# Gated DeltaNet layer of a decoder trunk: triangular inverse on 32- and 64-wide array tiles, decay rows by DRAM

## The chip, the cores and the metric

The kernel runs on one core of a Trainium2 chip. The metric is the device time of one execution in microseconds (us). The core has five engines with an instruction queue each: PE (matrix products; its weight loads are listed apart as PEld), DVE (vector), ACT (scalar functions), POOL (GpSimd) and SP (which here only issues DMAs). An engine works its queue in order.

## The reference

Four residual layers (mixers Mamba-2, HGRN2, Gated DeltaNet, Mamba-2), each followed by cross-attention into 256 memory tokens and a gated MLP; width 1024, 256 tokens, all float32. The change touches the third layer's mixer alone: 8 key heads, 16 value heads of 128, chunks of 64 tokens. Its core, shortened:

```
gc = cumsum(g)                                   # log decay within a chunk
decay = exp(where(incl, gc[l] - gc[s], -inf))
m = where(strict, (k * beta) @ k.T * decay, 0)
a_mat = m + I
sol = triangular_solve(a_mat, [v * beta, k * beta * exp(gc)])   # unit lower triangular
u, w = sol
att = (q @ k.T) * decay
per chunk: v_new = u - w @ state
           o = (q * exp(gc)) @ state + att @ v_new
           state = state * exp(gc_last) + (k * exp(gc_last - gc)).T @ v_new
```

## The kernel before

Tokens are handled as two chunks of 128, so a key head with its two value heads has four 128x128 triangular matrices (index `a`, two value heads by two chunks). All matrices of weights are float32 and are multiplied as three float32r products: `prep` (L152) loads a 128x1024 piece `raw` over SP's queue (four buffers), ACT casts it to `wH` (L160), DVE subtracts to get `wL` (L161), and `mm3` (L166) issues three matmuls with 256 moving columns for each 128x128 block. These projections fill PE. In the DeltaNet layer their outputs are `gps` (input projection, six column blocks a head) and `acc` (output projection).

The work of the heads is written as generators (`head`, L906) that are woven into this stream: `Weave` keeps a clock of PE time; each `yield cost, latency` adds the cost and says how much later the next step may stand. So the position of a step in PE's queue is set when the program is built, not on the chip. Up to three heads are under way at once.

One head does the following. It normalises q and k (`l2`, `kq`), broadcasts two rows of summed log decay over 128 partitions by a matmul with a selector (`grb`, L925: two float32r matmuls with 256 columns), forms the decays `E` (L930 to L933), the products `gp` (L942) and the scaled, masked matrices `MT` (L948) and `att`. `MT` goes to DRAM and its thirty-two 16x16 diagonal blocks come back as `blk` (L956, L957, both on SP's queue). POOL inverts these blocks in fifteen steps (L969, L971) and writes them by DMA into zeroed DRAM (L973); SP loads them as `U`, which is block diagonal (L987). That load stands in SP's queue among the loads of `raw`, and waits there until POOL's write has landed.

The inverse is then grown from blocks of 16 to 32 to 64 to 128. `U` is the transposed inverse, `Tm` the inverse. Four transposes make `Tm` from `U` (`tps`, L993). For each of two levels DVE masks `MT` to `ml` (L964), four 128x128 products give `yps` (L1000), ACT copies them to `Y` (L1005), four more give `ups` (L1009), DVE subtracts from `Tm` (L1011), four transposes (L1015) and an ACT copy (L1016) bring `U` up to date. The last level uses 64x64 products (L1021, L1028). A float32 product shows in the trace as two instructions (passes), a transpose or a float32r product as one. After this the head solves and runs the recurrence (`gvp`, `gsp`, `gs`, `grp`, `gop`, L1037 to L1087), normalises (`token_norm`) and transposes out (`gbp`, L1091).

## Time and profile before

| | |
|---|---|
| median of 3 runs | 2039.09 us (2039.07 to 2043.4) |
| the profiled execution | 2039.35 us |
| its span in the profile | 2037.6 us |
| DeltaNet mixer within the span | about 980 to 1288 us |
| PE busy, whole span | 98% |

The span is the time from the first to the last recorded instruction; 1.75 us of the profiled execution lie outside it. Busy time of PE counts a matmul from its start to the end of its passage through the array, and successive ones overlap, so what PE can deliver is read from the distance between starts, not from the busy share.

### The profile page before, as it was taken

The numbers are of one execution on the slowest core, as the hardware profiler recorded it, in microseconds if no ns is written. First come the engines' busy times: TensorE is split into PE (matmuls) and PEld (weight loads), VectorE is DVE, ScalarE is ACT, GpSimd is POOL, SyncE is SP. The second block draws the span as 40 slices with busy tenths as digits, with TensorE's granted clock in tenths as the row PEclk, the third lists the DMA queues.
The fourth block names the chain that finished last, engine by engine and source line by source line (L and its number), as shares of the span: only waits on it lengthen the run. The fifth ranks groups of instructions, "written<-read, shape, count | busy, mean of one in ns | idle before, by whom it ended". The sixth has DMA issues, their size and how long they took to land.

```text
span 2037.6 us, 42013 instructions
## 1 busy us (share of the span) xinstructions
PE 1987.2 (98%) x17020; PEld 1942.3 (95%) x17020; DVE 1575.0 (77%) x2417; ACT 1280.4 (63%) x1874; POOL 341.6 (17%) x468
## 2 busy tenths in 40 slices
PE   8999999999999999999999999999999999999997
PEld 8999999999999899999998899999999999999997
DVE  6899777875788778866786875878756999777875
ACT  6687666654565566555676875666545778666553
POOL 2032211000133110001064451110001133201001
PEclk9999999999999999999999999999999999999999
DMA  7655545666644546666544333457666565545663
GB/s 242 202 186 173 174 146 167 216 193 181 211 156 135 150 133 211 200 192 192 188 123 136 107 111 123 140 162 217 193 177 200 196 197 171 179 136 176 195 193 121
DMA packets 112770, 351.53 MB, mean 173 GB/s; under 512 B 15744, under 2 KB 25664, under 8 KB 112576
## 3 DMA queue, kind: packets, MB, share of 16 engines
q1 hardware_dynamic: 106176, 333.42, 52.9%
q10 hardware_dynamic: 6144, 15.17, 2.2%
q8 instruction: 133, 2.18, 0.4%
q0 software_dynamic: 256, 0.26, 0.1%
q14 instruction: 61, 0.50, 0.1%
HBM read 344.81 MB, written 4.00 MB: 171 GB/s over the span
## 4 chain that ended last, share of the span: by engine, by line
PE 78%; issue 5%; DVE 5%; ACT 4%; POOL 2%; DMA 1%; DVEq 0%; SPq 0%; POOLq 0%; ACTq 0%
PE ffps L170 8%; PE ffps L169 8%; PE ffps L168 8%; PE acc L168 6%; PE acc L169 6%; PE acc L170 6%; PE mps L168 4%; PE mps L170 3%; PE mps L169 3%; DVE wL L161 2%; PE qps L170 2%; PE qps L168 2%; PE qps L169 2%; PE kvps L168 1%; PE kvps L170 1%
## 5 line engine op out<-in xcount | busy, mean ns | idle before, releaser
L161 DVE TENSOR_TENSOR wL<-raw,wH 128x1024 fp32r<-128x1024 f32 (+2 forms) x639 | 786.3, 1232 | 326.8 <-ACT wH L160 324.3
L160 ACT CAST wH<-raw 128x1024 fp32r<-128x1024 f32 (+2 forms) x639 | 658.9, 1032 | 535.6 <-PE ffps L169 160.8
L168 PE MATMUL ffps<-hH,wH 128*128 128x256 f32 x1376 | 380.6, 277 | 0.0
L169 PE MATMUL ffps<-hL,wH 128*128 128x256 f32 x1376 | 379.8, 276 | 0.0
L170 PE MATMUL ffps<-hH,wL 128*128 128x256 f32 x1376 | 379.2, 276 | 0.0
L168 PE MATMUL acc<-aH,wH 128*128 128x256 f32 x1232 | 344.5, 280 | 0.0
L170 PE MATMUL acc<-aH,wL 128*128 128x256 f32 x1232 | 341.4, 277 | 0.6 <-DVE wL L161 0.6
L169 PE MATMUL acc<-aL,wH 128*128 128x256 f32 x1232 | 341.0, 277 | 0.0
L169 PEld LDWEIGHTS ffps<-hL,wH 128*128 128x128 f32 x1376 | 258.3, 188 | 0.1
L168 PEld LDWEIGHTS ffps<-hH,wH 128*128 128x128 f32 x1376 | 258.3, 188 | 0.1
L170 PEld LDWEIGHTS ffps<-hH,wL 128*128 128x128 f32 x1376 | 258.0, 188 | 0.0
L168 PEld LDWEIGHTS acc<-aH,wH 128*128 128x128 f32 x1232 | 231.5, 188 | 1.3 <-issue 0.7
L170 PEld LDWEIGHTS acc<-aH,wL 128*128 128x128 f32 x1232 | 231.3, 188 | 1.1 <-DVE wL L161 1.0
L169 PEld LDWEIGHTS acc<-aL,wH 128*128 128x128 f32 x1232 | 231.6, 188 | 0.6
L168 PE MATMUL mps<-hH,wH 128*128 128x256 f32 x768 | 218.0, 284 | 0.0
L169 PE MATMUL mps<-hL,wH 128*128 128x256 f32 x768 | 213.8, 278 | 0.0
L170 PE MATMUL mps<-hH,wL 128*128 128x256 f32 x768 | 213.0, 277 | 0.0
L212 POOL TENSOR_TENSOR ns<-nsq 128x256 f32<-128x256 f32 x13 | 10.7, 821 | 856.7 <-ACT nsq L209 856.7
L168 PEld LDWEIGHTS mps<-hH,wH 128*128 128x128 f32 x768 | 144.3, 188 | 2.9 <-issue 2.4
L169 PEld LDWEIGHTS mps<-hL,wH 128*128 128x128 f32 x768 | 144.4, 188 | 0.7
L170 PEld LDWEIGHTS mps<-hH,wL 128*128 128x128 f32 x768 | 144.4, 188 | 0.3
L170 PE MATMUL gps<-hH,wL 128*128 128x256 f32 x448 | 127.6, 285 | 0.6 <-DVE wL L161 0.6
(410 smaller groups left out, 4670.1 us busy)
## 6 DMA issues: line engine op xcount, KB each, us to landing
raw<-f_up SPq DMA_DIRECT2D x176, 512.0 KB, 4.1
raw<-m_in SPq DMA_DIRECT2D x96, 512.0 KB, 3.6
raw<-f_down SPq DMA_DIRECT2D x80, 512.0 KB, 4.2
raw<-xa_kv SPq DMA_DIRECT2D x60, 512.0 KB, 4.3
raw<-g_in SPq DMA_DIRECT2D x48, 512.0 KB, 4.1
raw<-m_out SPq DMA_DIRECT2D x32, 512.0 KB, 3.6
raw<-xa_q SPq DMA_DIRECT2D x32, 512.0 KB, 3.6
raw<-xa_o SPq DMA_DIRECT2D x32, 512.0 KB, 3.6
```

The costliest lines, as they stand in the source:

```text
L160: ACT.copy(H[:, c], raw[:, c])
L161: DVE.tensor_tensor(out=L[:, c], in0=raw[:, c], in1=f32(H[:, c]), op=ALU.subtract)
L168: PE.matmul(dst, aH, bH, start=start, stop=False, skip_group_check=True)
L169: PE.matmul(dst, aH, bL, start=False, stop=False, skip_group_check=True)
L170: PE.matmul(dst, aL, bH, start=False, stop=stop, skip_group_check=True)
L212: self.eng.tensor_tensor(out=self.sum, in0=sq[:, :T], in1=sq[:, T:], op=ALU.add)
```

## The change

The masks, the full-width products and the transposes of the two lower levels go. Products are now made only where blocks are: `MT`, `U` and `Tm` are cut into four groups of 32 partitions, and `block` (L1004 of the changed kernel) issues one small float32 product for each 32-partition group, so a product occupies a 32x32 tile of the array. `Tm` becomes a 128x4x64 tile and holds each half's 64x64 inverse in its own partitions; it is no longer made by transposing `U`. POOL makes a transposed copy of the inverted 16x16 blocks (`ut`), writes it to a third DRAM scratch, and SP loads `Tm` from there with two DMAs a head. Per head the two lower levels are: 16 products with 16 moving columns into `yps`, 12 and 16 products into `ups`, then 8 and 12 products of 32x32. The column `low`, zero or one by partition, takes the place of the mask. ACT writes pieces of `U` and DVE pieces of `Tm` straight from PSUM. The 64x64 level stays as it is.

The broadcast matmul `grb` goes too. The summed log decay rows `pk` are written to DRAM once (`grow`) on ACT's queue and each head's two rows are read back over 128 partitions by one DMA on ACT's queue, issued one head ahead (`fetch`).

By instruction counts over the eight heads: 96 transposes, 128 products of 128x128 and 16 of the broadcast leave PE; 512 small products come (128 with 32 weight columns and 16 moving, 96 of the same form, 128 with 16 and 16, 160 of 32x32). DVE loses 16 masks, 16 subtractions of 128x512 and 8 of 64x256, and gets 24 of 32x64 elements, 16 operations of 32x128 and 8 of 64x256. ACT loses 40 copies of 128x512 and gets 8 activations of 128x64, 48 of 16 or 32 partitions, 8 copies of 32x128 and 8 more loads of a function table. POOL gets 8 copies and 8 DMAs, SP 16 loads of `Tm` and 2 of zeros, ACT's queue 8 reads and 1 write of rows.

The core of the diff:

```diff
-            d = [[dr.tile([4, P + 1, P], F32, name=f"gd{i}{j}") for j in range(2)] for i in range(2)]
+            d = [[dr.tile([4, P + 1, P], F32, name=f"gd{i}{j}") for j in range(2)] for i in range(3)]
             for j in range(2):
-                nc.sync.dma_start(out=rows(d[1][j]), in_=zt)
+                for i in (1, 2):
+                    nc.sync.dma_start(out=rows(d[i][j]), in_=zt)
...
-            gcm = U1([P, 768], "gcm")
-            nc.scalar.dma_start(out=gcm, in_=io["cm"][:, CM["lvl"]:CM["lvl"] + 768])
+            gcm = U1([P, 512], "gcm")
+            nc.scalar.dma_start(out=gcm, in_=io["cm"][:, CM["i16"]:CM["i16"] + 512])
+            lvl, low = U1([P, P], "glvl"), U1([P, 1], "glow")
+            nc.scalar.dma_start(out=lvl, in_=io["cm"][:, CM["lvl"]:CM["lvl"] + P])
+
+            DVE.tensor_reduce(out=low, in_=lvl, axis=AX.X, op=ALU.max)
+            DVE.tensor_scalar(out=low, in0=low, scalar1=-1.0, scalar2=1.0, op0=ALU.mult, op1=ALU.add)
...
-                zero(rw)
-                DVE.tensor_copy(rw[:16], pk[:16])
-                DVE.tensor_tensor(out=rw[32:48], in0=pk[:16], in1=f32(rw[:16]), op=ALU.subtract)
+                nc.scalar.dma_start(out=rows_d, in_=pk[:16])
+
+            rbs = {}
+
+            def fetch(h):
+
+                rbs[h] = wk.tile([P, 2, T], F32, tag="grb", name="grb")
+                nc.scalar.dma_start(out=rbs[h], in_=bass.AP(tensor=rows_d.tensor, offset=rows_d.offset + 2 * h * T,
+                                                             ap=[[0, P], [T, 2], [1, T]]))
+
+            fetch(0)
 
             def columns():
                 tp = mx("gtp")
...
-                rb = mx("grb")
-                for j in range(2):
-                    hv = 2 * h + j
-                    PE.matmul(rb[:, j * T:(j + 1) * T], sel[:, hv:hv + 1].to_broadcast([P, P]), rw,
-                              start=j == 0, stop=True, skip_group_check=True)
+                rb = rbs[h]
+                if h < 7:
+                    fetch(h + 1)
...
-                ACT.activation(out=er, in_=rb.rearrange("p (j t) -> p j t", j=2)[:, :, P:], func=AF.Exp, scale=-1.0)
+                ACT.activation(out=er, in_=rb[:, :, P:], func=AF.Exp, scale=-1.0)
...
                 tm = wk.tile([32, 16, 16], F32, tag="tm", name="tm", bufs=1)
-                d0, d1 = scr[0][h % 2], scr[1][h % 2]
+                ut = wk.tile([32, 16, 16], F32, tag="ut", name="ut", bufs=1)
+                d0, d1, d2 = [s[h % 2] for s in scr]
                 nc.sync.dma_start(out=rows(d0), in_=MT)
...
-                ml = W(f"ml{h % 2}", 1)
-
-                def level(l):
-                    DVE.tensor_tensor(out=ml, in0=MT, in1=lvl[:, l:l + 1, :].to_broadcast([P, 4, P]), op=ALU.mult)
-
-                POOL.tensor_copy(ub.rearrange("p a b -> p (a b)"), gcm[:32, 256:512])
+                POOL.tensor_copy(ub.rearrange("p a b -> p (a b)"), gcm[:32, :256])
                 for j in range(15):
...
                 nc.gpsimd.dma_start(out=diag(d1), in_=ub)
+                POOL.tensor_copy(ut, ub.rearrange("p a b -> p b a"))
+                nc.gpsimd.dma_start(out=diag(d2), in_=ut)
...
                 nc.sync.dma_start(out=U, in_=rows(d1))
-                level(0)
+
+                Tm = wk.tile([P, 4, 64], F32, tag="Tm", name="Tm", bufs=2)
+                for b in (0, 64):
+                    nc.sync.dma_start(out=Tm[b:b + 64], in_=d2[:, b:b + 64, b:b + 64].rearrange("a s l -> s a l"))
                 yield 0, LAT[1]
-
-                tps = mx("tps")
+                Q = [slice(32 * i, 32 * i + 32) for i in range(4)]
+                quad = lambda ps, o, w: ps[:, o:o + 4 * w].rearrange("p (a b) -> p a b", a=4)
+
+                def block(d, lhsT, rhs, first):
+                    PE.matmul(d, lhsT, rhs, start=first, stop=True, skip_group_check=True)
+
+
+                ps = mx("yps")
+                yp = quad(ps, 0, 16)
                 for a in range(4):
-                    PE.transpose(tps[:, a * P:(a + 1) * P], U[:, a, :], ident)
-                Tm = W("Tm")
-                ACT.copy(flat(Tm), tps)
-                yield 440, LAT[2]
-                for l in range(2):
-                    yp = mx("yps")
-                    for a in range(4):
-                        PE.matmul(yp[:, a * P:(a + 1) * P], ml[:, a, :], Tm[:, a, :], start=a == 0, stop=True,
-                                  skip_group_check=True)
-                    if l == 0:
-                        level(1)
-                    Y = W("Y", 1)
-                    ACT.copy(flat(Y), yp)
-                    yield 870, LAT[3]
-                    up = mx("ups")
-                    for a in range(4):
-                        PE.matmul(up[:, a * P:(a + 1) * P], U[:, a, :], Y[:, a, :], start=a == 0, stop=True,
-                                  skip_group_check=True)
-                    DVE.tensor_tensor(out=flat(Tm), in0=flat(Tm), in1=up, op=ALU.subtract)
-                    yield 870, LAT[4]
-                    tps = mx("tps")
-                    for a in range(4):
-                        PE.transpose(tps[:, a * P:(a + 1) * P], Tm[:, a, :], ident)
-                    ACT.copy(flat(U), tps)
-                    yield 440, LAT[14]
-
-                yp = mx("yps")
+                    for i, q in enumerate(Q):
+                        block(yp[q, a], MT[q, a, q], Tm[q, a, 32 * (i % 2):32 * (i % 2) + 16], a == 0)
+                Y = wk.tile([P, 4, 16], F32, tag="Y0", name="Y0", bufs=1)
+                ACT.activation(out=Y, in_=yp, func=AF.Copy, scale=low)
+                yield 300, 1200
+                ps = mx("ups")
+                tp, up = quad(ps, 0, 16), quad(ps, 64, 16)
                 for a in range(4):
-                    PE.matmul(yp[64:, a * 64:(a + 1) * 64], MT[:64, a, 64:], Tm[:64, a, :64], start=a == 0, stop=True,
-                              skip_group_check=True)
-                Y = W("Y", 1)
-                ACT.copy(Y[64:, :, :64], yp[64:, :T].rearrange("p (a b) -> p a b", a=4))
-                yield 440, LAT[3]
-                up = mx("ups")
+                    for q in Q[:3]:
+                        block(tp[q, a], U[q, a, q], Y[q, a], a == 0)
                 for a in range(4):
-                    PE.matmul(up[:64, a * 64:(a + 1) * 64], Y[64:, a, :64], U[64:, a, 64:], start=a == 0, stop=True,
-                              skip_group_check=True)
-                DVE.tensor_tensor(out=U[:64, :, 64:], in0=U[:64, :, 64:], in1=up[:64, :T].rearrange("p (a b) -> p a b", a=4),
-                                  op=ALU.subtract)
-                yield 440, LAT[13]
+                    for i, q in enumerate(Q):
+                        block(up[32 * i:32 * i + 16, a], Y[q, a], U[q, a, 32 * i + 16:32 * i + 32], a == 0 and i == 3)
+                for i in (0, 2, 1):
+                    d = Tm[Q[i], :, 32 * (i % 2):32 * (i % 2) + 16]
+                    DVE.tensor_tensor(out=d, in0=d, in1=tp[Q[i]], op=ALU.subtract)
+                for i in (1, 3, 0, 2):
+                    ACT.activation(out=U[32 * i:32 * i + 16, :, 32 * i + 16:32 * i + 32], in_=up[32 * i:32 * i + 16], func=AF.Copy,
+                                   scale=-1.0)
+                yield 600, 1800
+
+                ps = mx("yps")
+                yp = quad(ps, 0, 32)
+                for a in range(4):
+                    for b in (0, 2):
+                        block(yp[Q[b + 1], a], MT[Q[b], a, Q[b + 1]], Tm[Q[b], a, :32], a == 0)
+                Y = wk.tile([P, 4, 32], F32, tag="Y1", name="Y1", bufs=1)
+                ACT.copy(Y[Q[1]], yp[Q[1]])
+                DVE.tensor_copy(Y[Q[3]], yp[Q[3]])
+                yield 300, 1200
+                ps = mx("ups")
+                tp, up = quad(ps, 0, 32), quad(ps, P, 32)
+                for a in range(4):
+                    block(tp[Q[1], a], U[Q[1], a, Q[1]], Y[Q[1], a], a == 0)
+                    for b in (0, 2):
+                        block(up[Q[b], a], Y[Q[b + 1], a], U[Q[b + 1], a, Q[b + 1]], a == 0)
+                DVE.tensor_scalar(out=Tm[Q[1], :, :32], in0=tp[Q[1]], scalar1=-1.0, scalar2=None, op0=ALU.mult)
+                for b in (2, 0):
+                    ACT.activation(out=U[Q[b], :, Q[b + 1]], in_=up[Q[b]], func=AF.Copy, scale=-1.0)
+                yield 400, 1500
+
...
```

PE's queue in the middle of the layer, with the inverses of two heads interleaved; `tps` are transposes, `yps` and `ups` the two products of a level, `l` and `grb` belong to the next head. Before:

```order
L1015 MATMUL tps<-ident,Tm 128x128 x4
L1000 MATMUL yps<-Tm,ml_13319 128x128 x4
L912 MATMUL l_13651<-gsq,ones 128x512
L925 MATMUL grb<-grw,sel 128x256 x2
L1000 MATMUL yps<-Tm,ml_13019 128x128 x4
L1009 MATMUL ups<-Y,U 128x128 x4
L170 MATMUL gps<-hH,wL 128x256
```

The same part of the layer in the changed kernel:

```order
L1004 MATMUL yps<-Tm,MT 64x64 x4
L168 MATMUL gps<-hH,wH 128x256
L169 MATMUL gps<-hL,wH 128x256
L170 MATMUL gps<-hH,wL 128x256
L168 MATMUL gps<-hH,wH 128x256
L169 MATMUL gps<-hL,wH 128x256
L1004 MATMUL ups<-Y_13732,U 32x16 x12
L1004 MATMUL ups<-U,Y_13732 16x16 x16
L923 MATMUL l_13814<-gsq,ones 128x512
L1004 MATMUL ups<-U,Y 64x64 x4
L1004 MATMUL yps<-Tm,MT 32x32 x8
```

Groups of four large products and of four transposes have become groups of 8 to 28 small ones, and the group of `grb` is gone. By the built program's tile sizes PE goes from 128-wide work to 32-wide tiles 38 times and back 40 times (two of the groups follow 64-wide ones).

SP's queue over the first two heads; the numbers behind `gd` tell scratch tensors apart. Before:

```order
L987 DMA U<-gd_12451 128x4x128
L159 DMA raw<-g_in 128x1024
L956 DMA gd_12450<-MT 128x4x128
L957 DMA blk<-gd_12450 32x16x16
L159 DMA raw<-g_in 128x1024 x3
L987 DMA U<-gd_12452 128x4x128
```

Now:

```order
L994 DMA U<-gd_12450 128x4x128
L966 DMA gd_12449<-MT 128x4x128
L998 DMA Tm<-gd_12452 64x4x64 x2
L967 DMA blk<-gd_12449 32x16x16
L159 DMA raw<-g_in 128x1024 x3
L994 DMA U<-gd_12451 128x4x128
L998 DMA Tm<-gd_12453 64x4x64 x2
```

Behind each load of `U` stand two of `Tm`, which wait for POOL's second write, and between the loads of `U` of these two heads there are three loads of `raw` instead of four.

## Rows read from the trace of the kernel before

**Rows 1.** The page's first part: busy time, share and instructions by engine.

```profile
PE 1987.2 (98%) x17020; PEld 1942.3 (95%) x17020; DVE 1575.0 (77%) x2417; ACT 1280.4 (63%) x1874; POOL 341.6 (17%) x468
```

**Rows 2.** Busy time by stretch, granted clock, DMA: the whole mixer, and ten microseconds in it.

```profile
980.40:1287.50 307.10, 294.87 (x2399) 278.45 (x2398) 229.48 (x433) 220.19 (x330) 117.81 (x269) 0.99 0.41 129
```

```profile
1070.00:1080.00 10.00, 6.81 (x33) 6.52 (x34) 4.67 (x8) 3.00 (x5) 4.74 (x15) 0.66 0.73 247
```

**Rows 3.** PE groups by line, 950 to 1400 us: count | busy, mean ns | idle before.

```profile
L1009 PE MATMUL ups<-Y,U 128*128 128x128 f32 x128 | 17.6, 281 | 0.1
L1000 PE MATMUL yps<-Tm,ml 128*128 128x128 f32 x128 | 17.1, 276 | 0.0
...
L1015 PE MATMUL tps<-ident,Tm 128*128 128x128 f32 x64 | 9.9, 278 | 0.1
...
L993 PE MATMUL tps<-ident,U 128*128 128x128 f32 x32 | 4.9, 274 | 1.2 <-DMA U<-gd 1.2
```

**Rows 4.** The chain of waits near its end in this layer: start, us, what.

```profile
1245.47 0.12 PE acc L168
1245.59 0.45 PE tps L1015 x4
1246.04 0.89 PE yps L1000 x8
1246.93 0.60 PE yps L1021 x8
```

**Rows 5.** Timeline of PE and of its weight loads around one 64x64 group.

```profile
1063.99 0.28 PE L170 MATMUL gps<-hH,wL 128*128 128x256 f32 x1
1064.20 0.67 PE L1028 MATMUL ups<-U,Y 64*64 64x64 f32 x8
1064.80 0.66 PE L1040 MATMUL gvp<-ident,vv 128*128 128x128 f32 x4
```

```profile
1064.19 0.54 PEld L1028 LDWEIGHTS ups<-U,Y 64*64 64x64 f32 x8
```

**Rows 6.** Weight loads by shape over the whole run, with their mean length.

```profile
L1028 PEld LDWEIGHTS ups<-U,Y 64*64 64x64 f32 x64 | 4.3, 134 | 1.2 <-ACT Y L1024 0.5
...
L759 PEld LDWEIGHTS op<-S,qd 128*32 128x32 f32 x112 | 3.0, 109 | 1.0
```

**Rows 7.** Timeline of PE around one broadcast of decay rows.

```profile
1044.11 0.80 PE L925 MATMUL grb<-grw,sel 128*128 128x256 f32 x2
1044.74 0.60 PE L993 MATMUL tps<-ident,U 128*128 128x128 f32 x4
```

**Rows 8.** SP's waits in the mixer (us, times, longest), and its timeline over the second head.

```profile
SPq L987 <- DMA gd<-ub: 86.2, 8, 16.9
```

```profile
1042.09 0.42 SPq L956 DMA_DIRECT2D gd<-MT  x1
1047.63 0.33 SPq L957 DMA_DIRECT2D blk<-gd  x1
1048.05 1.39 SPq L159 DMA_DIRECT2D raw<-g_in  x3
1066.36 0.38 SPq L987 DMA_DIRECT2D U<-gd  x1
```

**Rows 9.** Timelines of ACT and PE behind that load, with idle time and its releaser.

```profile
1071.37 1.04 ACT L160 CAST wH<-raw 128x1024 fp32r<-128x1024 f32 x1 [4.63 <-DMA raw<-g_in]
```

```profile
1073.11 1.22 PE L1064 MATMUL grp<-S,kd 128*128 128x128 f32 x4 [3.21 <-ACT S L1059]
```

**Rows 10.** Timeline of POOL at the end of one inversion of the 16x16 blocks.

```profile
1064.23 0.69 POOL L973 DMA_DIRECT2D gd<-ub  x1 [0.31 <-POOL ub L971]
1066.40 0.39 POOL L966 COPY ub<-gcm 32x256 f32<-32x256 f32 x1 [1.48 <-DMA gd<-ub]
```

**Rows 11.** Groups of ACT and of DVE in the mixer: count | busy, mean ns | idle before.

```profile
L1109 ACT ACT_TABLE_LOAD x7 | 9.0, 1283 | 2.2 <-DVE gc L331 2.1
```

```profile
L964 DVE TENSOR_TENSOR ml<-MT,gcm 128x512 f32<-128x512 f32 x16 | 11.0, 687 | 2.0 <-PE yps L1000 1.9
```

More of the change, by code (lines that the diff above doesn't have):

```diff
@@ L145, in tile_trunk @@
     DVE.memset(epsc, EPS)
-    sel = cst.tile([P, 32], F32R, name="sel")
+    cst.tile([P, 32], F32, name="cpad")
     rsmc = cst.tile([P, 2], F32, name="rsmc")
@@ L531, in softplus @@
         DVE.scalar_tensor_tensor(out=u, in0=u, scalar=0.0, in1=r, op0=ALU.max, op1=ALU.add)
-    def zero(t):
-        DVE.tensor_scalar(out=t, in0=ones[:, :1].to_broadcast([P, T]), scalar1=0.0, scalar2=None, op0=ALU.mult)
     def mamba(layer, ia, gname):
@@ L874, in gdn @@
             be = flat(be)[32:48]
-            (a, b), (c, d) = [[flat(t[:, :2]), flat(t[:, 2:])] for t in (U1([P, 4, P], "E"), U1([P, 4, P], "Y"))]
-            rw, tcol = U1([P, T], "grw", F32R), U1([P, 2, 64], "gtcol")
+            (a, b), (c, d) = [[t[:, 0, :], t[:, 1, :]] for t in (flat(U1([P, 4, P], "E")).rearrange("p (a b) -> p a b", a=2), U1([P, 2, T], "gsq"))]
+            tcol = U1([P, 2, 64], "gtcol")
+            rows_d = dr.tile([16, T], F32, name="grow")
             POOL.memset(pk, 0.0)
@@ L885, in gdn @@
                 DVE.tensor_scalar(out=ga, in0=ga, scalar1=na, scalar2=None, op0=ALU.mult)
-                DVE.tensor_tensor_scan(out=pk[:16], data0=gcm[:16, 512:768], data1=ga, initial=0.0,
+                DVE.tensor_tensor_scan(out=pk[:16], data0=gcm[:16, 256:512], data1=ga, initial=0.0,
                                        op0=ALU.mult, op1=ALU.add)
-                zero(rw)
-                DVE.tensor_copy(rw[:16], pk[:16])
-                DVE.tensor_tensor(out=rw[32:48], in0=pk[:16], in1=f32(rw[:16]), op=ALU.subtract)
+                nc.scalar.dma_start(out=rows_d, in_=pk[:16])
[5 more added lines that the diff above has]
+            fetch(0)
             def columns():
@@ L900, in gdn @@
             cols = weave.push(late(12000, columns()))
-            lvl = gcm[:, :2 * P].rearrange("p (a b) -> p a b", a=2)
             W = lambda nm, b=2: wk.tile([P, 4, P], F32, tag=nm, name=nm, bufs=b)
@@ L929, in head @@
                     for c in range(2):
-                        DVE.tensor_scalar(out=E[:, 2 * j + c, :], in0=rb[:, j * T + c * P:j * T + (c + 1) * P],
+                        DVE.tensor_scalar(out=E[:, 2 * j + c, :], in0=rb[:, j, c * P:(c + 1) * P],
                                           scalar1=tcol[:, c, 2 * h + j:2 * h + j + 1], scalar2=0.0,
@@ new lines, in head @@
+                for b in (2, 0):
+                    ACT.activation(out=U[Q[b], :, Q[b + 1]], in_=up[Q[b]], func=AF.Copy, scale=-1.0)
+                yield 400, 1500
+                ps = mx("yps")
+                yp = quad(ps, 0, 64)
+                for a in range(4):
+                    block(yp[64:, a], MT[:64, a, 64:], Tm[:64, a, :], a == 0)
+                Y = wk.tile([P, 4, 64], F32, tag="Y", name="Y", bufs=1)
+                ACT.copy(Y[64:], yp[64:])
+                yield 480, 1200
@@ L1034, in head @@
+                ps = mx("ups")
+                up = quad(ps, 0, 64)
+                for a in range(4):
+                    block(up[:64, a], Y[64:, a, :], U[64:, a, 64:], a == 0)
+                DVE.tensor_scalar(out=U[:64, :, 64:], in0=up[:64], scalar1=-1.0, scalar2=None, op0=ALU.mult)
+                yield 480, LAT[13]
                 while h not in vz or (h and h - 1 not in done):
@@ L1179, in tile_trunk @@
     nc.scalar.dma_start(out=cm, in_=io["cm"][:, :CM["bd"]])
-    DVE.tensor_copy(sel, cm[:, CM["sel"]:CM["sel"] + 32])
     st = Stats()
```

## The prediction

> **What bounds the kernel now.** I read the page's busy shares first: PE 98%, DVE 77%, ACT 63% [rows 1]. The PE share overstates, since passes overlap, so the next view is the busy time by stretch. Over the DeltaNet mixer PE is idle for 307.1 - 294.9 = 12.2 us [rows 2]; all other engines have room. Then the chain of waits: it steps from one PE instruction to the next without a gap, a projection pass 0.12 us, four transposes 0.45, eight passes of 128x128 products 0.89, eight passes of 64x64 products 0.60 [rows 4]. So in this layer almost everything that PE issues lies on the path, and the change is first of all an exchange of PE work. The latency of the inverse's chain matters little: of its steps only the first transposes show idle time before them, 1.2 us in eight heads [rows 3].
>
> There is one clear hole. SP holds each head's load of `U` until POOL's write has landed, 86.2 us over eight heads, at most 16.9 [rows 8]; the loads of `raw` stand behind it. After the longest hold ACT waits 4.63 us for `raw`, and PE 3.21 us [rows 9], and the ten microseconds around it have a mean granted clock of 0.66 of 2.4 GHz, part of them at the lower level, 1.2 GHz [rows 2].
>
> **PE work that goes.** Products of the two lower levels: 128 + 128 passes [rows 3] at 0.89 / 8 = 0.111 us [rows 4] are 28.4 us. Transposes: 64 + 32 [rows 3] at 0.45 / 4 = 0.1125 are 10.8 us. The broadcast: its two products and the way to the next instruction take 0.63 us at most, from start to start [rows 7], and two projection steps of 0.12 at least [rows 4]; since the product ahead still runs for part of the 0.63, I take 0.35, eight times 2.8 us. Together 42.0 us.
>
> **PE work that comes.** 512 small products are 1024 passes. What one costs is the term that decides, and no row shows a 32-wide product with few moving columns. A row for 64 does: eight weight loads of 134 ns mean [rows 6] take 0.54 us together [rows 5], so they are (0.54 - 0.134) / 7 = 58 ns apart. A 128-wide pass takes 111 [rows 4]. A straight line through the two has 0.83 ns a column and 5 ns besides, so 31 ns at 32 weight columns and 18 at 16. I take the line: 768 passes at 31 are 23.8 us, 256 at 18 are 4.6, together 28.4. The bounds are far apart. Above, 58 ns for each, the shortest distance that any row shows: 59.4 us. Below, four neighbouring products that sit on four different tiles pass at once, a quarter of 31: some 8 us.
>
> The Trainium skill, "TensorEngine Tiling (Array Packing)", section Instruction Overhead, states about 60 cycles for each matmul however few its columns. Worked out at 2.4 GHz that is an estimate of 25 ns, which would make the 256 narrowest passes 1.8 us dearer and PE's sum below -2.6 instead of -4.4; no run here shows it.
>
> **Going between tile sizes.** The built program goes to 32-wide tiles and back 40 times, mostly from and to 128-wide work. Rows have this for 64-wide groups: eight passes at 58 ns are 0.46 us, but the chain gives the group 0.60 [rows 4], so 0.14 is lost on the way out; on the way in the start stands 0.21 after the last projection pass instead of 0.12 [rows 5], another 0.09. 40 times 0.23 is 9.2 us. The 64-wide groups that remain pay this already.
>
> That the array empties at such a change is also the rule of the Trainium skill, "TensorEngine Tiling (Array Packing)", section Key Properties: "Mode switching requires drain". The trace agrees, with the 0.23 us above; a price of nothing would put PE's sum at -13.6 us.
>
> PE's exchange is therefore -42.0 + 28.4 + 9.2 = -4.4 us.
>
> **SP, POOL and the new waits.** Each head adds on POOL a copy (0.39 us, by the copy of the same size) and a DMA (0.69) [rows 10], so the second write lands some 1.1 us after the first. SP then issues two loads of `Tm` at about 0.4 each [rows 8], so `raw` is held about 1.9 us longer a head. Behind the wait for `Tm` stand the next head's write of `MT`, its `blk` read and three loads of `raw`; who waits for these are ACT's casts and then PE. At the hole above there is now one `raw` fewer ahead of the hold, 24 passes of 0.12 or 2.9 us of cover. Against that, the read of `blk` no longer has a 512 KB load ahead of it: its write took 1042.09 to 1047.63 to be waited out [rows 8], and half of these 5.5 us may go, so POOL starts some 2.7 us sooner. That leaves +2 us at this hole. At the other seven holds no PE wait of this size stands behind, so I put them at nothing: the four `raw` buffers cover them. Without that cover they cost up to 1.9 each (below).
>
> **ACT and DVE.** DVE is relieved of two masks of 0.69 us a head [rows 11] and as many full-width subtractions, against some six small operations; ACT's smaller copies are paid back by one more table load of 1.28 us a head [rows 11]. The rows are fetched a head ahead on ACT's queue, behind no wait that is not long over except the first, which follows the write of the rows by several ACT instructions. Both engines have over 75 us idle in the mixer [rows 2]; cost nothing, and a gain of at most a part of the 12.2 us, of which I take 1.5, about the wait that the first transposes had.
>
> **The sum.** 2039.35 (the profiled execution, 0.26 above the median of the runs) - 4.4 + 2 - 1.5 = 2035.5; forecast 2035.
>
> **Rivals.**
> *Tiles side by side.* Neighbouring products of a group sit on different tiles. If they overlap, a pass costs between 8 and 31 ns. For it: on one 64-wide tile a load and a product already overlap, since a load alone takes 134 ns and the pair 58 [rows 5, 6]. Against: all eight of that group use one tile, so no row shows two at work. At 16 ns: 16.4 us instead of 28.4, 2023; at 8 ns 2015. The Trainium skill, "TensorEngine Tiling (Array Packing)", section Key Properties, says that different tiles load and multiply in parallel; no run here shows it yet.
>
> *A floor under a small pass* (the other sign). If the 58 ns are mostly not columns but the price of one load and one product, 1024 passes cost up to 59.4 us and the time is 2066; at 45 ns, 46.1 us, it is 2053. PE breaks even at (42.0 - 9.2) / 1024 = 32 ns, and the kernel is measurably slower from about 36 ns. For it: a weight load only shrinks from 134 to 109 ns between 64 and 32 columns [rows 6], so most of it is fixed. Against: that fixed part is hidden at 64 columns.
>
> *SP's hold starves PE in every head.* 1.9 us, eight times, 15 us, and some at the lower clock: 2035 + 17 = 2052. It decides once the hold outlasts the loaded `raw` in more than two or three heads. For it: holds of 86.2 us in eight [rows 8] and the hole of rows 9. Against: one such hole in eight heads.
>
> *The small products still occupy the whole array*, 111 ns a pass: 114 us, 2121. The tile sizes in the built program speak against it.
>
> **How the numbers follow.** A measurement of this kernel can tell about 0.2%, 4 us: faster is under 2035.0, slower over 2043.2. Forecast 0.42 (own range 2029 to 2042; faster 0.20, same 0.20, slower 0.02); tiles side by side 0.27, all faster; floor 0.17 (slower 0.14, same 0.03); starving 0.12 (slower 0.09, same 0.03); whole array 0.02, slower. Faster 0.47, same 0.26, slower 0.27. The range 2018 to 2058 leaves out the far ends of the two rivals on the pass, about 0.07 each, and the last case.
>
> **What would show it.** In the changed profile: the distance of small passes in PE's timeline (31 and 18 ns, or 16, or 45 and more); the way in and out of a 32-wide group, 0.23 us together; idle time of PE behind SP's holds, with SP's wait for the load of `Tm` about 1 us behind that for `U`; eight more table loads on ACT at no PE wait. I am wrong if a pass is far from the line, if the change of tile size costs otherwise at 32 than at 64, or if PE's idle time in the mixer passes 15 us.

## The result, and the profile after

The changed kernel takes 2075.23 us (median of 4 runs, 2067.19 to 2078.95), the kernel before on the same chip 2041.24: a ratio of 1.0153, 95% interval 1.0108 to 1.0198. It is slower by 1.5%; 2035 was forecast, at most 2058. The profiled execution is the fastest of the four; it has a span of 2065.4 us, 27.8 more than before, so what the profile accounts for is 27.8 us and not the 34 between the medians. The first part of its page reads

```profile
PE 1989.8 (96%) x17676; PEld 1939.4 (94%) x17676; DVE 1562.1 (76%) x2423; ACT 1286.1 (62%) x1906; POOL 346.2 (17%) x484
```

Against [rows 1] little seems to have happened. The busy time by stretch shows where to look: the mixer (start and end; length; busy time of PE, PEld, DVE, ACT, POOL; granted clock; DMA), then 20 us in it.

```profile
980.60:1308.60 328.00, 289.30 (x3055) 266.73 (x3055) 218.30 (x439) 226.10 (x363) 121.91 (x285) 0.93 0.44 134
```

```profile
1040.00:1060.00 20.00, 13.43 (x175) 11.80 (x174) 11.88 (x23) 9.06 (x15) 14.05 (x33) 0.83 0.45 131
```

Against [rows 2] the mixer is 328.0 - 307.1 = 20.9 us longer, PE is idle in it for 38.7 us instead of 12.2, and the granted clock is 0.93 instead of 0.99. In the trace's stretches of clock, 44.4 us of the mixer are at 1.2 GHz, where 6.8 were before. Some 7 us more lie in the last gated MLP; they are another matter (below, the two paces).

PE's waits in the mixer (engine and line, for whom; us in total, times, longest):

```profile
PE yps L1004 <- DMA Tm<-gd: 15.3, 9, 6.0
PE grp L1095 <- ACT S L1090: 4.8, 1, 4.8
PE gbp L1122 <- DVE on L835: 3.9, 3, 2.0
PE gop L1114 <- DVE vtok L1105: 3.5, 1, 3.5
```

The longest of them, in PE's timeline:

```profile
1041.72 0.28 PE L169 MATMUL gps<-hL,wH 128*128 128x256 f32 x1
1041.84 1.02 PE L923 MATMUL l<-gsq,ones 128*128 128x512 f32 x2
1048.87 0.29 PE L1004 MATMUL yps<-Tm,MT 32*32 32x16 f32 x4 [6.01 <-DMA Tm<-gd]
1049.72 0.61 PE L1004 MATMUL yps<-Tm,MT 32*32 32x16 f32 x28 [0.56 <-DMA Tm<-gd]
...
1051.71 0.41 PE L170 MATMUL gps<-hH,wL 128*128 128x256 f32 x1
1051.92 0.41 PE L168 MATMUL gps<-hH,wH 128*128 128x256 f32 x1
...
1053.83 0.28 PE L168 MATMUL gps<-hH,wH 128*128 128x256 f32 x1
1053.95 0.28 PE L169 MATMUL gps<-hL,wH 128*128 128x256 f32 x1
```

PE has nothing to do for 6 us, because the next instruction in its queue is a small product and its `Tm` has not landed. Then the projection goes at 0.21 us a step instead of 0.12, until 1053.83. So this wait costs 6.6 us in two pieces, and the 4.4 us of work behind it, at the lower clock, some 2 more. What it waited for is in POOL's and SP's timelines:

```profile
1042.53 0.86 POOL L978 DMA_DIRECT2D gd<-ub  x1 [0.32 <-POOL ub L976]
1043.39 0.63 POOL L979 COPY ut<-ub 32x256 f32<-32x256 f32 x1
1044.32 0.66 POOL L980 DMA_DIRECT2D gd<-ut  x1 [0.30 <-POOL ut L979]
```

```profile
1044.84 0.38 SPq L994 DMA_DIRECT2D U<-gd  x1
1045.31 0.46 SPq L966 DMA_DIRECT2D gd<-MT  x1
1046.47 1.33 SPq L998 DMA_DIRECT2D Tm<-gd  x2
```

PE reached the product at 1042.9, before POOL had even issued the second write. The new path is one to two microseconds longer than the old one, but most of the 6 us is that both ends moved: POOL's inverse is 3.6 us later in this head than before, counted from the mixer's first product, and PE is some 2 us earlier.

**Where the time went.** Adding the distances between the starts of PE's instructions in the mixer, less its idle time, separately by granted clock:

| mixer of | idle | at 2.4 GHz | at 1.2 GHz | sum |
|---|---|---|---|---|
| before | 12.2 | 288.4 | 6.2 | 306.8 |
| changed | 38.7 | 248.4 | 40.6 | 327.7 |

Counting what ran at 1.2 GHz half, PE's work is 291.5 us before and 268.7 after: 22.8 us less. Idle time takes back 26.5, the lower clock 17.2 (20.3 - 3.1). The sum is +20.9. The change does more for PE than was forecast (22.8 us instead of 4.4), and PE then stands still for longer than it saved.

### The profile page after: what moved, and what is told of

It reads as the page before. It is cut to its first block, busy times and chain, and to the rows that moved or that the text cites. A ratio compares the mean times of both kernels' runs of the same rounds, so it can differ in the third digit from the quotient of the medians.

```text
span 2065.4 us, 43402 instructions
## 1 busy us (share of the span) xinstructions
PE 1989.8 (96%) x17676; PEld 1939.4 (94%) x17676; DVE 1562.1 (76%) x2423; ACT 1286.1 (62%) x1906; POOL 346.2 (17%) x484
## 4 chain that ended last, share of the span: by engine, by line
PE 76%; issue 6%; DVE 5%; POOL 4%; ACT 3%; DMA 3%; SPq 0%; DVEq 0%; POOLq 0%; ACTq 0%
PE ffps L169 8%; PE ffps L168 8%; PE ffps L170 8%; PE acc L168 6%; PE acc L169 6%; PE acc L170 6%; PE mps L168 3%; PE mps L170 3%; PE mps L169 3%; DVE wL L161 2%; PE qps L170 2%; PE qps L169 2%; PE qps L168 2%; PE kvps L168 1%; PE kvps L169 1%
## 5 line engine op out<-in xcount | busy, mean ns | idle before, releaser
L212 POOL TENSOR_TENSOR ns<-nsq 128x256 f32<-128x256 f32 x13 | 10.4, 801 | 862.3 <-ACT nsq L209 862.3
```

What stands on the lines that cost most here:

```text
L212: self.eng.tensor_tensor(out=self.sum, in0=sq[:, :T], in1=sq[:, T:], op=ALU.add)
```

## The experiments

Times of whole runs turned out to be a blunt measure, since the projections have two paces (last experiment). The mixer of the profiled execution is therefore compared first: its length, PE's idle time in it (both from the busy time by stretch), and the time in it at 1.2 GHz. "Rest" is the span less the mixer. Each kernel of the table is explained in its place below. A mixer length is that of one execution; two pairs that differ by 128 bytes of address (before and before_shifted, rows_only and rows_padded) agree within 0.8 us, which is the only measure of its scatter.

| kernel | mixer | idle | at 1.2 GHz | rest | median | ratio to before, interval |
|---|---|---|---|---|---|---|
| before | 307.1 | 12.2 | 6.8 | 1730.5 | | |
| changed | 328.0 | 38.7 | 44.4 | 1737.4 | 2075.2 | 1.0153 (1.0108 to 1.0198) |
| rows_only | 322.9 | 22.4 | 20.5 | 1767.7 | 2092.1 | 1.0246 (1.0222 to 1.0269) |
| rows_padded | 323.5 | 26.5 | 13.7 | 1730.2 | 2062.5 | 1.0075 (1.0035 to 1.0115) |
| inverse_only | 331.3 | 35.6 | 61.4 | 1755.4 | 2066.0 | 1.0136 (1.0075 to 1.0197) |
| tm_by_pe | 323.3 | 28.2 | 41.0 | 1737.6 | 2063.5 | 1.0092 (1.0058 to 1.0125) |
| small_tiles_only | 316.6 | 24.9 | 34.1 | 1731.0 | 2048.0 | 1.0032 (1.0006 to 1.0059) |
| small_tiles_late | 327.0 | 29.6 | 44.4 | 1738.6 | 2066.7 | 1.0107 (1.0065 to 1.0149) |
| tm_later | 325.0 | 36.8 | 41.0 | 1729.7 | 2058.4 | 1.0086 (1.0058 to 1.0113) |
| changed_slack | 344.4 | 50.4 | 64.9 | 1730.9 | 2078.6 | 1.0162 (1.0110 to 1.0214) |
| tm_pe_slack | 334.2 | 38.6 | 47.8 | 1757.5 | 2088.0 | 1.0184 (1.0117 to 1.0250) |
| fill_wait | 337.7 | 35.8 | 47.8 | 1737.5 | 2078.1 | 1.0161 (1.0102 to 1.0220) |
| before_early | 336.7 | 36.9 | 27.3 | 1736.9 | 2073.4 | 1.0149 (1.0095 to 1.0203) |
| u_on_pool | 307.1 | 22.8 | 13.7 | 1746.2 | 2052.9 | 1.0009 (0.9989 to 1.0029) |
| changed_on_pool | 341.1 | 45.5 | 75.1 | 1746.1 | 2079.7 | 1.0143 (1.0107 to 1.0179) |
| rows_u_on_pool | 325.4 | 32.2 | 37.5 | 1745.6 | 2068.9 | 1.0090 (1.0054 to 1.0126) |
| u_on_pool_08 | 304.9 | 16.2 | 20.5 | 1730.3 | 2044.6 | 0.9998 (0.9973 to 1.0023) |
| u_on_pool_16 | 317.1 | 27.7 | 27.3 | 1740.0 | 2058.9 | 1.0070 (1.0038 to 1.0103) |
| before_shifted | 306.3 | 11.3 | 3.4 | 1767.5 | 2076.6 | 1.0152 (1.0113 to 1.0191) |

### Each part alone

The theory at first was that the loss is the path of `Tm`, and that the decay rows are innocent.

> The kernel before with the decay rows alone taken from DRAM; the inverse stays as it was. Theory (the loss is the path of Tm: POOL's transposed copy, the second scratch write, two loads on SP): this part is innocent, 8 broadcast products fewer, so -3 to 0 us, 2036 to 2041. Rival (the rows come late or their reads collide with the weight stream): most of the loss is here, 2060 to 2075.

```diff
-                rb = mx("grb")
-                for j in range(2):
-                    hv = 2 * h + j
-                    PE.matmul(rb[:, j * T:(j + 1) * T], sel[:, hv:hv + 1].to_broadcast([P, P]), rw,
...
+                rb = rbs[h]
```

The mixer is 15.8 us longer, by the rows alone, and the rest 37 us longer although nothing there was changed. (This kernel keeps the rows in one buffer, the changed one in two; no engine waits for the rows of a later head.) So that the mixer can be judged apart, the run was made again with the selector's 128 bytes left free:

> The run rows_only again, with 128 bytes left free at the place of the selector that it no longer needs, so that all later tiles lie at the addresses that they have in the kernel before. In rows_only the projections outside the mixer ran at 117.8 ns a matmul instead of 113.3, and 37 of its 52 us lay outside the mixer. Theory A (the addresses set this pace): the stretches outside the mixer return to 980.6 and 742.6 us, the time is about 2050 to 2058 with the mixer still 12 to 16 us longer. Theory B (the pace is settled at random or by something else): 2080 to 2095 again. Theory on the mixer (PE comes to the load of U earlier since work is gone, waits, and the clock falls): mixer 315 to 323 us. Rival (rows_only's mixer was slow by its pace alone): mixer 304 to 310.

The rest returns to 1730.2, the mixer stays at 323.5. The decay rows are not innocent: they cost 16.4 us of mixer.

```profile
979.90:1303.40 323.50, 296.97 (x2384) 279.65 (x2383) 226.13 (x429) 229.87 (x337) 124.30 (x269) 0.98 0.42 129
```

The largest single wait comes from head 0. DVE's decays `E`, before and then in rows_padded:

```profile
1010.76 1.12 DVE L930 TENSOR_SCALAR E<-grb,gtcol 128x128 f32<-128x128 f32 x4
```

```profile
1015.13 0.87 DVE L936 TENSOR_SCALAR E<-grb,gtcol 128x128 f32<-128x128 f32 x4 [0.40 <-DMA grb<-grow]
```

and ACT's queue in rows_padded, which writes the rows and reads them back:

```profile
1006.29 0.33 ACTq L891 DMA_DIRECT2D grow<-gpk  x1
1010.24 0.33 ACTq L898 DMA_DIRECT2D grb<-grow  x1
```

The read of the first head's rows is issued 4 us after the write, behind a cast and two loads of a function table, and lands 4.9 us later. Counted from the mixer's start, `MT` of head 0 is done 2.9 us later than before (40.5 instead of 37.6) and SP issues the load of its `U` 5.9 later (66.4 instead of 60.5). Head 0's chain is the one that has no other head's work in front of it, and PE meets it:

```profile
1049.49 1.12 PE L1001 MATMUL tps<-ident,U 128*128 128x128 f32 x4 [5.52 <-DMA U<-gd]
```

There was no wait at this place before [rows 7]. These 5.5 us are shown to come from the late rows. The other 9 us of new idle time stand at later steps, and without the broadcast products the order of PE's steps has moved too (head 1's first transposes stand behind 606 projection passes instead of 630), so how much of the 16.4 us is the rows' way and how much the order is not separated.

> The changed kernel with the broadcast products put back: the change of the inverse alone. Theory (path of Tm): as slow as the changed kernel or 3 us slower, 2070 to 2080, with PE idle about 35 to 40 us in the mixer. Rival (the rows by DMA are at fault): 2035 to 2045.

The other part alone: the mixer takes 331.3, with PE waiting 18.9 us for `Tm`; the median, 2066.0, lies below the 2070 to 2080 expected.

```profile
PE yps L997 <- DMA Tm<-gd: 18.9, 10, 6.8
```

Both parts cost alone, 16.4 and 24.2 us, and 20.9 together: they don't add. What the rows cost depends on what stands around them: fetching them by DMA makes the mixer 16.4 us longer here, 6.7 longer with the small tiles and `Tm` made by PE (small_tiles_only to tm_by_pe), 18.3 longer with `U` on POOL's queue, and 3.3 shorter in the changed kernel (inverse_only to changed). That both parts make PE wait in the same places would explain it; it is argued, not shown.

### The way of Tm

> The changed kernel, but Tm is made of U by four PE transposes and two ACT copies, as before; the transposed copy on POOL, the second scratch write and the two Tm loads are gone, the small tiles and the rows by DMA stay. Theory (path of Tm): PE no longer waits for Tm, 32 transposes come back (3.6 us), the waits of 15.3 us and the low clock behind them go: 2020 to 2035, below before. Rival A (the small passes and the switches of tile size cost more than they save): still 2060 to 2080. Rival B (the short chain of the inverse meets its latency in any case, now on U): 2040 to 2060, with PE's waits moved to the first small product or the transposes.

```diff
-                for b in (0, 64):
-                    nc.sync.dma_start(out=Tm[b:b + 64], in_=d2[:, b:b + 64, b:b + 64].rearrange("a s l -> s a l"))
...
+                tps = mx("tps")
+                for a in range(4):
+                    PE.transpose(tps[:, a * P:(a + 1) * P], U[:, a, :], ident)
+                t4 = tps.rearrange("p (a t) -> p a t", a=4)
+                for b in (0, 64):
+                    ACT.copy(Tm[b:b + 64], t4[b:b + 64, :, b:b + 64])
```

A miss: 4.7 us of mixer come back, not 20 or more. PE now waits for `U` (8.1 us) and at four other places. With the rows put back as well, the small tiles stand alone:

> The kernel before with the small tiles alone: the decay rows are broadcast by PE as before, Tm is made of U by four PE transposes as before, the products of the two lower levels run on 32-wide tiles. No DMA, no POOL work and no wait is added. Theory (both DMA detours delay the chain of MT, U and Tm by 4 to 8 us, PE comes early and waits, and each wait costs as much again at the lower clock): head 0's U lands near 63 us after the mixer's start as before, idle in the mixer under 20 us, half clock under 20 us, mixer 290 to 303 us, time 2025 to 2038, below before. Rival (any work taken from PE makes it early at the latencies of the chain, whatever the path): idle 25 us or more, mixer 308 to 325, 2042 to 2060.

316.6 us, in the range of the rival (308 to 325).

```profile
980.50:1297.10 316.60, 291.66 (x3103) 268.01 (x3102) 219.37 (x443) 222.08 (x372) 110.51 (x269) 0.95 0.41 126
```

So with the rows on PE, the detour of `Tm` costs 331.3 - 316.6 = 14.7 us, against 4.7 with the rows by DMA. But even the small tiles alone, with no DMA added and less work for PE, are 9.5 us slower than before. The waits of this run:

```profile
PE tps L997 <- DMA U<-gd: 7.8, 3, 3.8
PE grp L1091 <- ACT S L1086: 6.5, 1, 6.5
PE gp L944 <- DVE kq L921: 3.3, 3, 1.6
```

### Moving PE's place in the order

If PE is early, the first small product could stand later in its queue. The pauses are numbers of the planner: the latencies in `Weave`'s table, in nanoseconds.

```diff
-    LAT = [21000, 5620, 1450, ...
+    LAT = [21000, 9620, 1450, ...
```

> The changed kernel with the pause between the load of U and the first small product 4.0 us longer in the planner's clock (9.62 instead of 5.62 us), so that the product stands later in PE's queue. Theory (path of Tm is late by 1.7 us in the mean, 6.0 at most): the 15.3 us of waits for Tm fall under 4 us and the clock stays high: 2045 to 2058. Rival A (price of small passes and switches): no change, 2070 to 2080. Rival B (SP's queue holds the weights, not Tm): PE waits for the projection's weights instead, 2065 to 2080.

The waits for `Tm` are gone, and 3.0 of the 20.9 us, but 41.0 us are still at 1.2 GHz. One wait of 9.2 us, PE behind `S` behind ACT's cast of `raw`, is new in size, and five of `gbp`. Three more moves of this kind:

> The changed kernel with longer pauses: 4.0 us more ahead of the load of U, 4.0 ahead of the first small product, 2.0 ahead of the last transposes, 0.8 ahead of gp. In tm_later the one wait that grew was PE behind ACT's cast of raw, 9.2 us, held by SP's wait for U's and Tm's scratch. Theory (SP's hold ends when its wait for the scratch is short): that wait falls under 4 us, mixer 303 to 315, 2040 to 2055. Rival (waits only move): mixer 322 to 330, 2055 to 2068.

> tm_by_pe with longer pauses in the planner: 4.0 us more ahead of the load of U, 1.5 more ahead of its first use, 2.0 more ahead of the last transposes, 0.8 more ahead of the gp products; the shorter chain of the inverse leaves room for this. Theory (PE's saved work of some 22 us is given back because PE, early, waits 28 us and then runs at the lower clock for 41 us): idle in the mixer under 18 us, half clock under 20 us, mixer 300 to 312 instead of 323, time 2035 to 2052. Rival (the waits only move to other places): mixer 318 to 326, 2058 to 2066.

> small_tiles_only with the first use of U 2.5 us later in the planner's clock. Theory: waits for U go, if there are any left; mixer within 5 us of small_tiles_only. Rival (early PE): the waits at U go and the mixer is 5 to 12 us shorter than small_tiles_only.

All three made the mixer longer, by 16.4, 10.9 and 10.4 us against the run they start from; the theory behind their numbers fell. A pause ahead of the load of `U` (in the first two) delays the load as well as PE, and in the woven order the steps move in leaps, not by the amount of the pause. How strongly that works was measured on the kernel before itself:

> The kernel before with one number changed: the first use of U stands 2.0 us earlier in the planner's clock; no operation, transfer or address changes. Theory (PE early at U waits and then loses the clock): 5 to 12 us of waits at the first transposes of U, half clock from 7 to 20 us or more, mixer 312 to 324 instead of 306.8. Rival (before has slack at this place, and the losses of the changed kernel come from its transfers): mixer 305 to 309, within 3 us of before.

```diff
-    LAT = [21000, 5620, 1450, ...
+    LAT = [21000, 3620, 1450, ...
```

Not an operation differs, and the mixer is 29.6 us longer, beyond the 312 to 324 us that the theory gave and more than by the whole change:

```profile
980.40:1317.10 336.70, 299.81 (x2398) 282.47 (x2398) 227.90 (x432) 229.35 (x338) 115.75 (x269) 0.96 0.38 118
```

```profile
PE tps L993 <- DMA U<-gd: 23.4, 5, 12.2
PE gps L170 <- DVE wL L161: 3.9, 2, 3.3
```

In the built program head 0's first transposes stay where they were, behind 445 projection passes of the mixer, but head 1's move from 630 passes to 499. PE stands before them for 12.2 us. So the place of these steps decides over as much time as the change does; the order before fits its own latencies, with 1.2 us of waits for `U` [rows 3].

The lower clock after the waits was tried by filling the wait with work:

```diff
+                fill = mx("tps")
+                for a in range(16):
+                    PE.transpose(fill[:, a % 4 * P:(a % 4 + 1) * P], MT[:, a % 4, :], ident)
```

> The changed kernel with work added: 16 transposes of MT that nobody reads, 1.8 us, ahead of the first small product of each head, where PE waits for Tm. Theory (the lower clock after these waits costs about as much as the waits): the added 14.4 us of PE work fit into the 15 us of waits, the 44 us at half clock fall to 15 to 30, and the mixer is no longer than 327.7 us in spite of the added work, 318 to 328. Rival (the clock has no part; the fill lands in part where PE does not wait): mixer 331 to 340 us.

A miss: 9.7 us longer, as the rival had it, and 47.8 us at the lower clock. The waits for `Tm` are 20.9 us now, since the order moved again. That the lower clock costs 17 us is a sum from the trace; that it could be avoided by such filling is not shown.

### SP's queue

In small_tiles_only and in the kernel before, SP holds `U`'s load until POOL's write has landed, and the next head's `MT` and the loads of `raw` stand behind it [rows 8]. u_on_pool takes that hold away and leaves PE's order as it is, but for one swap of neighbouring passes; `U` gets a third buffer.

```diff
                 nc.gpsimd.dma_start(out=diag(d1), in_=ub)
+                U = W("U", 3)
+                nc.gpsimd.dma_start(out=U, in_=rows(d1))
...
-                U = W("U")
-                nc.sync.dma_start(out=U, in_=rows(d1))
```

> small_tiles_only, with the load of U issued on POOL's queue right behind POOL's write, instead of on SP's (one buffer of U more). PE's order is the same, instruction by instruction. Theory (the inverse's chain is late because SP holds: the next head's write of MT and the loads of raw stand behind the wait for U): SP's hold of 80 to 90 us for U is gone, the solves of heads 1 and 2 start 5 to 9 us earlier, PE's waits behind S (6.5 us) and U (7.8 us) go, idle in the mixer under 15 us, half clock under 15 us, mixer 290 to 302 instead of 316.3, time 2020 to 2034, below before. Rival (POOL's own wait for its write delays the next solves as much): mixer 312 to 325.

9.5 us come back: the mixer is as long as before, 307.1 us.

```profile
988.40:1295.50 307.10, 284.31 (x3103) 260.64 (x3102) 220.31 (x442) 221.96 (x372) 116.33 (x277) 0.98 0.44 130
```

POOL's inversions of heads 1 and 2 begin 6.6 and 13.5 us earlier, the wait behind `S` is gone, and the time at 1.2 GHz falls from 34.1 to 13.7. The load itself is slower from this queue (5.3 us to landing in head 0 instead of 2.8), so 10.8 us of waits for `U` remain. That SP's hold takes part in the loss of this kernel is shown in the profiled executions, since PE's order is the same; the ratios of the whole runs, 1.0009 against 1.0032, differ by less and their intervals overlap. The range given, 290 to 302, was not reached.

> The changed kernel with the loads of U and Tm on POOL's queue right behind POOL's writes (three buffers of U and Tm). Theory (SP's hold and the late Tm cause most of the loss): Tm lands 2 to 8 us earlier from head 1 on, waits for Tm under 6 us instead of 15.3, mixer 303 to 315 instead of 327.7, time 2040 to 2055. Rival (the losses are PE's early order alone, wherever the loads stand): mixer 322 to 335.

For the changed kernel itself the same move fails: 341.1 us, with 32.1 us of waits for `Tm`. `Tm` lands 3.2 us later in head 0 than in the changed kernel, but 2.3 of them are there already when POOL writes the inverted blocks (64.1 us after the mixer's first product instead of 61.8), before any of the moved loads. PE's order moved too, so this run doesn't separate the causes.

> tm_by_pe with the load of U on POOL's queue: small tiles, Tm by PE, rows by DMA. Against u_on_pool this adds the rows by DMA alone. Theory (the rows' way through DRAM delays head 0's MT by 3 to 5 us and with it U): PE waits for head 0's U 3 to 5 us, mixer 4 to 10 us longer than u_on_pool in spite of 4.8 us less PE work. Rival (with U early, the rows' delay is covered): mixer 2 to 6 us shorter than u_on_pool.

The rows by DMA on top of u_on_pool cost 18.3 us, about as in rows_padded, more than expected; with 6.7 us of wait for head 0's `U`. This run is also tm_by_pe with the load of `U` moved, and PE's order is again the same but for one swap of passes. Here the move gains nothing: 323.3 us before it, 325.4 after, and the waits for `U` grow from 8.1 to 16.8 us. So what SP's hold costs is shown with the rows on PE alone.

> u_on_pool with the first use of U 0.8 us later in the planner's clock (6.42 instead of 5.62 us). In u_on_pool four waits for U are left, 2.5, 3.1, 4.0 and 1.1 us, the first with PE 2.5 us early. Theory (PE's place against U decides): head 0's wait goes, as its first transposes now stand 22 projection passes later (2.5 us); the waits for U fall under 6 us, mixer 298 to 306. Rival (the planner's table is tuned so closely that any move costs): mixer 308 to 322.

> u_on_pool with the first use of U 1.6 us later in the planner's clock. Theory: the waits for U are gone but for 2 us; later steps of the chain may now be the late ones: mixer 295 to 308. Rival (any move costs): 310 to 325.

A pause of 0.8 us more gives the shortest mixer of all, 304.9, and no difference in time from before: 0.9998. By the sum over starts this kernel has some 13 us less PE work than before (it makes `Tm` by transposes and keeps the broadcast); the best order found here keeps two of them. A pause of 1.6 us more gives 317.1, as the rival had it: 10 us longer than without the pause.

### The two paces of the projections

rows_only had lost 37 us where nothing was changed. The busy time by stretch, of the same 80 us in a stretch of nothing but projections, in the kernel before and in rows_only:

```profile
400.00:480.00 80.00, 80.00 (x708) 80.00 (x708) 57.35 (x74) 42.55 (x55) 0.00 (x0) 1.00 0.66 194
```

```profile
400.00:480.00 80.00, 80.00 (x681) 80.00 (x681) 57.22 (x75) 42.09 (x55) 0.00 (x0) 1.00 0.61 186
```

708 passes against 681, at the same granted clock: 113 and 117.5 ns a pass. That the addresses of the tiles do this was tried on the kernel before:

```diff
-    sel = cst.tile([P, 32], F32R, name="sel")
...
+            sel = U1([P, 32], "gsel", F32R)
```

> The kernel before; its selector of 128 bytes lies in the mixer's own pool instead of among the constants, so that the tiles of all other layers lie 128 bytes lower, as they do in rows_only. No other operation changes. Theory A (addresses set the projections' pace): outside the mixer 996 to 1002 and 755 to 763 us instead of 980.6 and 742.6, 2070 to 2085 in all. Theory B (the pace comes from elsewhere): as before, 2037 to 2056.

All four runs lie between 2075.6 and 2076.7, the mixer is 306.3, the rest 37 us longer:

```profile
400.00:480.00 80.00, 80.00 (x682) 80.00 (x681) 57.20 (x75) 42.03 (x55) 0.00 (x0) 1.00 0.59 185
1900.00:1980.00 80.00, 80.00 (x682) 80.00 (x681) 63.74 (x90) 42.43 (x60) 0.00 (x0) 1.00 0.61 189
```

So tiles that lie 128 bytes lower bring the slower pace, and 1.5%; rows_only and rows_padded, which differ in these bytes alone, say the same. The changed kernel keeps the selector's place free (`cpad`), and is not hit by this as a whole. But the pace can change without it: in the changed kernel's profile it falls in the last MLP (681 passes in 1900 to 1980 us, 709 before), in tm_later's, with the same addresses there, it doesn't (708). What sets it there is open. It is a likely reason, not a shown one, for the spread of the kernel before: 2036.9 to 2064.0 us over all its runs, 1.3%.

## Why the prediction was wrong

*PE work that goes*: 42.0 us was about right. The sum over starts has 22.8 us less work, which with the 20 us of the next point makes 43.

*PE work that comes*: mis-sized, on the good side. The line was to give 31 and 18 ns a pass and the groups to pay 0.23 for tile sizes. PE's timeline of the changed kernel:

```profile
1135.29 0.43 PE L1004 MATMUL yps<-Tm,MT 32*32 32x16 f32 x28
1135.65 0.71 PE L1102 MATMUL gsp<-vtok,U 128*128 128x128 f32 x4
...
1137.68 0.28 PE L170 MATMUL gps<-hH,wL 128*128 128x256 f32 x1
1137.89 0.40 PE L1004 MATMUL ups<-Y,U 32*32 32x16 f32 x21
1138.12 0.18 PE L1004 MATMUL ups<-U,Y 32*16 32x16 f32 x1
1138.13 0.19 PE L1004 MATMUL ups<-Y,U 32*32 32x16 f32 x3
1138.16 0.41 PE L1004 MATMUL ups<-U,Y 32*16 32x16 f32 x31
1138.50 0.71 PE L1114 MATMUL gop<-vtok,gatt 128*128 128x128 f32 x4
```

28 passes take 0.36 us, 56 take 0.61, way out included: 13 and 11 ns. The way in costs 0.21 instead of 0.11, so 0.10. Over eight heads the 32-wide groups take some 16 us (22.9 at the full clock and 5.3 at half, counted 2.65, for all of `yps` and `ups`, less 16 groups of 0.60 for the 64-wide level), and 40 ways in some 4 more, together 20 and not 28.4 + 9.2. PE's exchange was -22.8 us instead of -4.4. The rival of tiles side by side had the mechanism and the price, 8 to 31 ns a pass. The Trainium skill, "TensorEngine Tiling (Array Packing)", section Key Properties, says that tiles work in parallel, and the trace agrees: 11 to 13 ns. The floor of about 60 cycles a matmul that the Trainium skill states on the same page, section Instruction Overhead, an estimate of 25 ns, does not hold for neighbours on different tiles: 11 to 13 ns here. Of the 0.23 us for a change of tile size 0.10 is seen on the way in, little on the way out.

*SP, POOL and the new waits*: this step failed. +2 us at one hole and nothing at the other seven was the sum; PE's idle time rose by 26.5. Of these, 14.1 stand where PE takes the fresh inverse (15.3 for `Tm`, where 1.2 for `U` were); the rest is spread over other steps of the heads (4.2 behind `Y`, where nothing was, 3.5 behind `vtok`, 4.8 instead of 3.2 behind `S`), which the step did not price. Part of it is mis-sized prices: POOL's copy takes 0.63 us, up to 1.38, not 0.39; SP's two loads take 1.33, not 0.8; its wait for the second write adds 12.7 us in eight heads. The larger part is that the step asked for SP's cover, the four `raw` buffers, and not for PE's. What stands next in PE's queue is the small product itself, and its cover was thin: before, `U` landed 0 to 3.2 us ahead of PE's first transposes in six heads, 6.8 and 17.6 in the other two. In the six, what POOL and SP come later, or PE comes earlier, beyond that is a wait. That an earlier PE is enough for it, before_early shows: 23.4 us of waits for `U`, with not an operation changed.

*ACT and DVE: cost nothing.* This failed as well. "Behind no wait that is not long over except the first" named the place, and put no price on it: the first rows come 4.9 us late, and PE waits 5.5 us for head 0's `U` (rows_padded, whose mixer is 16.4 us longer in all). The gain of 1.5 us, taken for the wait of the first transposes, went the other way: that wait is the 15.3 us above.

*The lower clock* had no term of its own. It comes with the waits and takes back 17.2 of the 22.8 us that PE's work fell by.

*The rivals* were taken as alternatives, each with its own time. In the run tiles side by side held (below the forecast), and waits that no rival had in full came on top (above it). The two are not independent: what PE saves makes it earlier at the place where it waits. SP's hold as the rival told it, PE starved of `raw` in every head, is not in the changed trace: ACT waits 10.9 us for `raw`, in two places, where it waited 9.8 in four, and PE stands behind such a wait once, for 4.8 us (3.2 before). "The latency of the inverse's chain matters little" was read from a trace in which PE came late enough. The condition "wrong if PE's idle time passes 15 us" was the right one. What a measurement can tell, "0.2%, 4 us", was set too fine: the interval of the result is 0.9% wide.

What stays open: how the 20.9 us divide between the two detours, since alone they cost 16.4 and 24.2; how much of each wait is a late operand and how much an early PE; and whether another order would keep more of the 22.8 us. Of seven moves of the planner's numbers five made the mixer longer.

## What to carry to other kernels

When work is taken from the engine that bounds a kernel whose order is fixed when it is built, look at what stands next in that engine's queue and how long before it its operand lands; if that is short, as the 0 to 3.2 us here, the saving can become a wait, as it did here, and with the wait came the lower clock. A detour through DRAM is priced on the head of the pipeline, where nothing covers it, not on the mean. Before a difference of 1% is put down to a change, compare stretches that the change doesn't touch: if they differ, the rest is not the change.

## What the runs showed of the hardware

Small float32 passes on neighbouring 32-wide tiles go 11 to 13 ns apart, a tenth of a 128-wide one. The stretches at 1.2 GHz lie at PE's waits: each of the eight in the changed mixer begins during a PE wait of 1.6 to 6.0 us or at most 1.6 us after its end. The first begins inside the 6.01 us wait above and lasts 6.8 us, so most of it falls on work. And the projections' stream has two paces, 113 and 117.5 ns, at a granted clock of 1.00: with the tiles 128 bytes lower the slower one held in both stretches shown, for 37 us in all.
